# Layer 1's sliding-window attention: the attention sink as a 193rd score column in a fixed tile per group, and the exponentials of a step issued in two halves

## The chip, the cores and the metric

The kernel runs on one core of one Trainium2 chip. The metric is the device time of one execution in microseconds (us). Before the change it is 2704.29 us, the median of 3 runs (2703.48 to 2707.02). A difference of about 0.2%, some 5.4 us, is the least that a measurement of this kernel can tell from none.

A core has five engines that run their own instruction queues in order and wait for each other by semaphores: TensorE (PE in the profile; PEld is its weight load), VectorE (DVE), ScalarE (ACT), GpSimd (POOL) and SyncE (SP), which here only issues DMAs. Matmuls write to PSUM, an accumulator memory of 8 banks; everything else lives in SBUF, the on-chip working memory.

## The reference, cut to what matters

The program is one inference step of a two-layer encoder on 2048 prompt frames and 64 sample frames. The change touches only layer 1, a sliding-window attention with 16 query heads over 2 key/value heads. Each chunk of 64 frames reads itself and the two chunks before it, so at most 192 keys. Each head has a learned sink: one more column of the softmax, with a constant score and no value.

```python
def _grouped_attend(q, k, v, valid, scale, bias=None, sinks=None):
    s = jnp.einsum('...qhgd,...khd->...hgqk', q, k).astype(jnp.float32) * scale
    s = jnp.where(valid, s, NEG_INF)
    if sinks is not None:
        hk, g = q.shape[-3], q.shape[-2]
        sk = jnp.broadcast_to(sinks.astype(jnp.float32).reshape(hk, g, 1, 1), s.shape[:-1] + (1,))
        p = jax.nn.softmax(jnp.concatenate([s, sk], axis=-1), axis=-1)[..., :-1]
    return jnp.einsum('...hgqk,...khd->...qhgd', p.astype(v.dtype), v)

def _c_layer(h, pos, cache, pre_g, post_g, w_in, sinks, w_out):
    ...
        o = _band_prompt(q, k, v, C_PAST_CHUNKS, C_SCALE, sinks=sinks)
    ...
    return h + _rms((o * jax.nn.silu(g)) @ w_out, post_g), state
```

## The kernel before

The program runs five phases one after the other: projections of layer 0, its two attentions, its output projection, the projections of layer 1 (phase 4) and, last, `phase5`: layer 1's attention and output projection. Matmuls use a pair of numbers (a high part and a remainder) for each operand, so many tiles come as `hi` and `lo`: `copy` (L211, on ACT) rounds a PSUM tile to its high part, and `lo_of` (L214, on DVE) subtracts that from the PSUM tile for the remainder.

**Units.** `phase5` works in 64 units: 16 blocks of 128 frames, in each two chunks (`ch`), in each two groups (`g`) of 8 heads. A unit holds 4 score pictures `c` of 128 rows (2 heads by 64 frames) by up to 192 keys. Its life, in the methods of `Soft` and `Unit`:

- `score`: 8 matmuls into the PSUM tile `s` (L1697; two banks, a pool of two such tiles used in turn), then on DVE the row maximum (L1699), the smaller of its negative and the negative sink (L1700, into `m[:,1]`), and sink minus maximum (L1701, into `m[:,2]`).
- `exp`: 4 exponentials on ACT with row sums (L1708, 192 columns each), then one small exponential of the 4 sink terms (L1711).
- `divide`: on DVE the sum plus the sink's term (L1715), a reciprocal (L1716), and the product of `P` and it (L1717).
- `turn`: 4 transposes on PE (L1723), the ACT copy (L211), and behind it the DVE remainder (L214). There are two turns in a unit, 128 keys and 64 keys.
- `av`: 4 matmuls with the values into `acc` (L1730). `out`: ACT copies the upper half of `acc` to `tbm` (L211), and two DVE additions (L1818) write `OT`.

**The output projection** runs between them. When a block's four units are out, `gate` multiplies `OT` by the gate on POOL (L1740), copies it to `MM` on ACT (L211), and subtracts for the remainder on POOL (L1747). `pump` then issues the projection's matmuls (L964) in small portions; ACT copies the result to `z` (L211) and sums its squares (L983); POOL and DVE work out the norm's factor (L987, L186 on POOL, L187 and L188 on DVE, L192 to L197 on POOL); DVE scales `z` in two halves (L995), and POOL adds the residual (L1003).

**Order.** Step `n` of the loop interleaves four units: `n+2` is scored (`ahead`), `n` is turned (`cur`), `n+1` is divided (`nxt`) and `n-1` gets its values and goes out (`prv`). The first 8 steps (`NAUTO5`) are left to a scheduler, which orders each engine's queue by a planned timeline; from step 8 on, the queues of PE, DVE, ACT and SP stand as the code is written, and only POOL's is planned. The heart of a step:

```python
for b in range(2):
    ...
        PT, low = cur.turn(*parts[b][:2])
    ...
    pump(RATE5 / 2)
    if low:
        low()
    if b == 0 and prv:
        prv.av()
    if b == 0 and nxt:
        nxt.divide()
    if b == 0 and prv:
        prv.out()
if ahead:
    ahead.exp([0, 1, 2, 3])
```

The sample's 64 frames form two more units (`sample`), which run their own `score`, `exp` and `divide` among the first steps, with tiles from the same pools.

Of the kernel before, what the change touches and what calls it, by code (L numbers as in the profile page):

```python
# [7 lines left out]
F32 = mybir.dt.float32  # L8
# [3 lines left out]
ALU = mybir.AluOpType  # L12
# [98 lines left out]
def kernel(ctx, tc, a, o, upto=5):  # L111
# [1555 lines left out]
    def phase5():  # L1667

        with ExitStack() as st:
# [8 lines left out]
            sink = row_bcast(one, a["c_sinks"], 16, "sink")  # L1678

            ssink = one.tile([128, 8], F32, name="ssink")  # L1680
            nssink = one.tile([128, 8], F32, name="nssink")
            for e in range(2):
                nc.vector.tensor_copy(ssink[e * 64:e * 64 + 64], sink[e * 64:e * 64 + 64].rearrange("p (j e) -> p j e", e=2)[:, :, e])
            nc.vector.tensor_scalar(nssink, ssink, -1.0, None, op0=ALU.mult)
            class Soft:


                def score(self, lhs, widths, w, g):
                    self.w = w
                    js = slice(g * 4, g * 4 + 4)  # L1690
                    s = self.s = ps_s.tile([128, 4, 256], F32, name="s")
                    m = self.m = sc.tile([128, 3, 4], F32, name="m", bufs=4)
                    for c in range(4):
                        o0 = 0
                        for wd, kk in widths:
                            for x in range(2):
                                nc.tensor.matmul(s[:, c, o0:o0 + wd], lhs(c), kk[x], start=(x == 0), stop=(x == 1))  # L1697
                            o0 += wd
                    nc.vector.tensor_reduce(m[:, 0], s[:, :, :w], axis=AX.X, op=ALU.max)  # L1699
                    nc.vector.scalar_tensor_tensor(m[:, 1], m[:, 0], -1.0, nssink[:, js], op0=ALU.mult, op1=ALU.min)  # L1700
                    nc.vector.tensor_tensor(m[:, 2], m[:, 1], ssink[:, js], op=ALU.add)  # L1701

                def exp(self, cs):
                    m, w = self.m, self.w
                    if cs[0] == 0:
                        self.P = pp.tile([128, 4, 192], F32, name="P")
                    for c in cs:
                        nc.scalar.activation(self.P[:, c, :w], self.s[:, c, :w], AF.Exp, bias=m[:, 1, c:c + 1],  # L1708
                                             accum_out=m[:, 0, c:c + 1])
                    if cs[-1] == 3:  # L1710
                        nc.scalar.activation(m[:, 2], m[:, 2], AF.Exp)  # L1711

                def divide(self):
                    m, w = self.m, self.w
                    nc.vector.tensor_tensor(m[:, 0], m[:, 0], m[:, 2], op=ALU.add)  # L1715
                    nc.vector.reciprocal(m[:, 0], m[:, 0])  # L1716
                    nc.vector.tensor_tensor(self.P[:, :, :w], self.P[:, :, :w], m[:, 0, :, None].to_broadcast([128, 4, w]),  # L1717
                                            op=ALU.mult)

                def turn(self, k0, kk):  # L1720
                    t = ps_t.tile([128, 512], F32, name="t")
                    for c in range(4):
                        nc.tensor.transpose(t[:kk, c * 128:c * 128 + 128], self.P[:, c, k0:k0 + kk], ident)  # L1723
                    PT = ppt.tile([128, 2, 512], F32R, name="PT")
                    copy(PT[:kk, 0], t[:kk])
                    return PT, lambda: lo_of(PT[:kk, 1], t[:kk], PT[:kk, 0])
# [163 lines left out]
            def step(n):  # L1890
# [10 lines left out]
                for b in range(2):  # L1901
# [10 lines left out]
                        nxt.divide()  # L1912
                    if b == 0 and prv:
                        prv.out()
                if ahead:
                    ahead.exp([0, 1, 2, 3])
                if prv:
                    us.pop(n - 1)
                    if n % 4 == 0 and n // 4 + 1 in blocks and n > 0:
# [128 lines left out]
```

## Time and profile before

| | |
|---|---|
| median of 3 runs | 2704.29 us |
| the profiled execution: its time, its span (first to last instruction) | 2703.56 us, 2701.8 us |
| mean granted TensorE clock | 0.986 |
| `phase5`, from its first score to the end of the span | 2237 us to 2701.8 us |
| of it planned by the scheduler (8 steps) / in written order (56 steps and the rest) | to some 2300 us / from there |
| a block (4 steps) in the written order, from one matmul to the same one a block later | 25.8 us |

The page of the profile gives the busy time of each engine and the costliest groups of instructions. The timeline lists instructions of one engine in order: start, duration, engine, source line, operation, tiles written and read, and in brackets the idle time ahead of the instruction with what ended it. The table by stretches gives, for each stretch, its length and then the busy time of PE, PEld, DVE, ACT and POOL, the granted clock and the DMAs' share. In the list of waits each row is the waiting engine and line, what it waited for, the sum, the number of times and the longest.

### The profile page before, as it was taken

To read this page: it belongs to the slowest core of one execution; us is meant where nothing else is said; L and a number is where in the kernel's file an instruction comes from. 1 tells how busy PE (TensorE), PEld (TensorE's weight loads), DVE (VectorE), ACT (ScalarE), POOL (GpSimd) and SP (SyncE) were. 2 spreads that over 40 slices of the span, in tenths; PEclk is the share of its full clock that TensorE was granted. 3 is DMA by queue.
4 is the path that set the end of the run, shared out by engine and by line. 5 is a ranking of instruction groups with operands and counts; after the bars stand their busy time and mean duration, and the time that the engine had idled before them with its cause. 6 is when DMAs were issued, how large, how long until landed. Compare 5 with 4: busy or idle time off the path is not lost.

```text
span 2701.8 us, 46285 instructions
## 1 busy us (share of the span) xinstructions
PE 2564.7 (95%) x16160; PEld 2311.6 (86%) x16160; DVE 1602.8 (59%) x4111; ACT 1359.8 (50%) x3516; POOL 502.5 (19%) x970
## 2 busy tenths in 40 slices
PE   6999999999999999999999999899999998989987
PEld 6999999899998888888778887789999997767765
DVE  6553345453227878787668776474214116899996
ACT  4332242422337777777667666443223214766663
POOL 0001000001002323311201333421001000344443
PEclk9999999999999999999899999999999998999999
DMA  7546443737537666661478776566426349466552
GB/s 241 169 152 209 125 152 115 253 105 226 165 103 206 181 180 191 168 165 48 169 210 191 204 203 185 177 238 209 148 76 191 105 101 235 98 143 132 132 123 74
DMA packets 416760, 438.89 MB, mean 162 GB/s; under 512 B 116224, under 2 KB 343368, under 8 KB 413296
## 3 DMA queue, kind: packets, MB, share of 16 engines
q1 hardware_dynamic: 416528, 435.93, 55.9%
q8 instruction: 129, 2.11, 0.3%
q14 instruction: 103, 0.84, 0.1%
HBM read 283.78 MB, written 157.09 MB: 163 GB/s over the span
## 4 chain that ended last, share of the span: by engine, by line
PE 72%; DVE 14%; ACT 6%; DMA 4%; issue 2%; POOL 1%; SPq 0%; ACTq 0%; DVEq 0%; POOLq 0%
PE pm L237 38%; PE proj L964 8%; PE s L683 6%; PE acc L754 4%; DVE PT L214 3%; PE t L726 3%; PE acc L1228 3%; PE s L1176 2%; PE t L1203 2%; DVE z L995 1%; DVE P L1717 1%; ACT P L702 1%; DVE m L689 1%; POOL x L1003 1%; PE t L1723 1%
## 5 line engine op out<-in xcount | busy, mean ns | idle before, releaser
L237 PE MATMUL pm<-X,W 128*128 128x384 f32 (+2 forms) x4536 | 751.9, 324 | 1.9 <-ACT X L211 1.0
L237 PEld LDWEIGHTS pm<-X,W 128*128 128x128 f32 x4536 | 729.8, 189 | 4.8 <-ACT X L211 1.7
L211 ACT ACTIVATE PT<-t 128x512 fp32r<-128x512 f32 (+3 forms) x704 | 344.9, 504 | 238.0 <-PE t L1203 76.2
L214 DVE SCALAR_TENSOR_TENSOR PT<-t,PT 128x512 fp32r<-128x512 f32 (+4 forms) x688 | 378.8, 569 | 87.7 <-ACT PT L211 83.8
L964 PE MATMUL proj<-Wo,MM 128*128 128x512 f32 (+1 forms) x1440 | 401.3, 408 | 5.6 <-ACT z L211 4.6
L964 PEld LDWEIGHTS proj<-Wo,MM 128*128 128x128 f32 (+1 forms) x1440 | 249.4, 187 | 55.6 <-ACT z L211 8.8
L214 DVE SCALAR_TENSOR_TENSOR ev<-pm,ev 128x256 fp32r<-128x256 f32 (+3 forms) x197 | 98.6, 503 | 334.0 <-ACT ev L430 100.2
L237 PE MATMUL pm<-W,X 128*128 128x256 f32 (+5 forms) x2040 | 281.2, 297 | 0.0
L237 PEld LDWEIGHTS pm<-W,X 128*128 128x128 f32 (+1 forms) x2040 | 272.0, 187 | 1.1
L702 ACT ACTIVATE P<-s,m 128x512 f32<-128x512 f32 (+9 forms) x344 | 209.6, 616 | 33.0 <-DVE m L691 30.4
L683 PE MATMUL s<-KA,Q 128*128 128x512 f32 (+7 forms) x640 | 201.4, 397 | 9.3 <-ACT P L702 8.4
L228 DVE TENSOR_TENSOR W<-R,W 128x768 fp32r<-128x768 f32 (+3 forms) x114 | 116.2, 1055 | 133.0 <-ACT W L227 132.5
L689 DVE TENSOR_REDUCE m<-s 128x1 f32<-128x480 f32 (+7 forms) x216 | 132.4, 613 | 80.6 <-PE s L683 80.3
L726 PE MATMUL t<-ident,P 128*128 128x128 f32 x1088 | 176.4, 276 | 3.4 <-ACT P L702 0.6
L726 PEld LDWEIGHTS t<-ident,P 128*128 128x128 f32 x1088 | 134.6, 141 | 41.6 <-ACT P L702 15.1
L754 PE MATMUL acc<-PT,V 128*128 128x256 f32 x1152 | 156.0, 285 | 6.6 <-DVE OT L763 6.6
L754 PEld LDWEIGHTS acc<-PT,V 128*128 128x128 f32 x1152 | 140.4, 188 | 12.0 <-PE t L726 6.0
L211 ACT ACTIVATE tbm<-acc 64x512 f32<-64x512 f32 (+1 forms) x136 | 77.5, 570 | 117.8 <-PE acc L1730 86.3
L1228 PE MATMUL acc<-PT,V 128*128 128x256 f32 x672 | 111.5, 298 | 6.5 <-DVE OT L1238 4.3
L683 PE MATMUL s<-KR,Q 128*128 128x384 f32 (+6 forms) x320 | 116.2, 363 | 1.2 <-DMA Q<-sQR 1.2
L1180 DVE CUSTOM_DVE_ANT_0 s<-s,bias 128x640 f32<-128x640 f32 (+4 forms) x128 | 95.2, 744 | 35.0 <-PE s L1176 33.5
L227 ACT ACTIVATE W<-R 128x768 fp32r<-128x768 f32 (+3 forms) x114 | 98.2, 909 | 29.6 <-DMA R<-in_ab_w_in_dram 13.0
(238 smaller groups left out, 3907.3 us busy)
## 6 DMA issues: line engine op xcount, KB each, us to landing
Q<-sQA SPq DMA_DIRECT2D x128, 128.0 KB, 3.2
sWO<-W SPq DMA_DIRECT2D x32, 512.0 KB, 3.8
Q<-sQB SPq DMA_DIRECT2D x128, 128.0 KB, 3.2
Wo<-sWO SPq DMA_DIRECT2D x16, 1024.0 KB, 8.8
Q<-sQC SPq DMA_DIRECT2D x64, 256.0 KB, 6.3
R<-in_ab_w_in_dram SPq DMA_DIRECT2D x40, 384.0 KB, 3.9
K<-sKB SPq DMA_DIRECT2D x56, 256.0 KB, 5.4
V<-sVB SPq DMA_DIRECT2D x24, 512.0 KB, 6.6
```

The lines of the kernel that those rows point to most:

```text
L211: nc.scalar.activation(out, in_, AF.Copy)
L214: nc.vector.scalar_tensor_tensor(out, x, scale, hi, op0=ALU.mult, op1=ALU.subtract)
L227: nc.scalar.activation(Wv[:, 0, k0:k1], Rv, AF.Copy)
L228: nc.vector.tensor_tensor(Wv[:, 1, k0:k1], Rv, Wv[:, 0, k0:k1], op=ALU.subtract)
L237: nc.tensor.matmul(ps, lhs(x, k), rhs(y, k), start=(j == 0), stop=(j == n - 1))
L683: nc.tensor.matmul(s[:r, :n], self.Q[:, x, self.qo:self.qo + r], rhs, start=(x == 0), stop=(x == 2))
L689: nc.vector.tensor_reduce(m[:r, j:j + 1], s[:r, :n], axis=AX.X, op=ALU.max)
L702: nc.scalar.activation(self.P[:r, o0:o0 + n], self.s.pop(j)[:r, :n], AF.Exp, bias=self.m[:r, 6:7], accum_out=acc)
L726: nc.tensor.transpose(t[:, b], self.P[:, (b0 + b) * 128:(b0 + b + 1) * 128], ident)
L754: nc.tensor.matmul(acc[:, (i // 2) % 2], H.V[:, b0 + b], PT[:, x, b], start=(b0 + b == 0 and x == 0), stop=(b0 + b == i and x == 1))
L964: nc.tensor.matmul(p, M[:, x, k, :r], W[k][:, y, cs], start=(k == k0 and t == 0), stop=(k == k1 - 1 and t == 2))
L1228: nc.tensor.matmul(acc, self.H.V[:, self.base - self.H.b0 + b], self.PT[:, x, off + b], start=(b == 0 and x == 0), stop=(b == nblk - 1 and ...
```

## The change

The sink becomes part of the score tile. Two fixed PSUM tiles `S_[g]`, one for each group, take the place of the pool's two tiles in turn. Column 192 of each is filled once with the group's sinks; scores are written right-aligned ahead of it, from column `k0 = 192 - w`. The maximum is taken over the scores and the sink together and written with its sign turned; each exponential covers 193 columns, so its row sum holds the sink's term. `nssink`, L1700, L1701, L1711 and L1715 go. `P` gets rows of 193 elements, of which the product covers the 192 without the sink's. And `ahead.exp` moves into the loop over `b`: two of the four exponentials at the end of each half of a step.

```diff
@@ phase5
             ssink = one.tile([128, 8], F32, name="ssink")
-            nssink = one.tile([128, 8], F32, name="nssink")
...
-            nc.vector.tensor_scalar(nssink, ssink, -1.0, None, op0=ALU.mult)
+
+            S_ = [ps_s.tile([128, 4, 256], F32, name=f"s{g}", bufs=1) for g in range(2)]
+            for g in range(2):
+                nc.vector.tensor_copy(S_[g][:, :, 192:193], ssink[:, g * 4:g * 4 + 4, None])
+
             class Soft:
                 def score(self, lhs, widths, w, g):
-                    self.w = w
-                    js = slice(g * 4, g * 4 + 4)
-                    s = self.s = ps_s.tile([128, 4, 256], F32, name="s")
-                    m = self.m = sc.tile([128, 3, 4], F32, name="m", bufs=4)
+                    self.k0 = 192 - w
+                    s = self.s = S_[g]
+                    m = self.m = sc.tile([128, 2, 4], F32, name="m", bufs=4)
                     for c in range(4):
-                        o0 = 0
+                        o0 = self.k0
...
-                    nc.vector.tensor_reduce(m[:, 0], s[:, :, :w], axis=AX.X, op=ALU.max)
-                    nc.vector.scalar_tensor_tensor(m[:, 1], m[:, 0], -1.0, nssink[:, js], op0=ALU.mult, op1=ALU.min)
-                    nc.vector.tensor_tensor(m[:, 2], m[:, 1], ssink[:, js], op=ALU.add)
+                    nc.vector.tensor_reduce(m[:, 1], s[:, :, self.k0:193], axis=AX.X, op=ALU.max, negate=True)
                 def exp(self, cs):
...
-                        self.P = pp.tile([128, 4, 192], F32, name="P")
+                        self.P = pp.tile([128, 4, 193], F32, name="P")
                     for c in cs:
-                        nc.scalar.activation(self.P[:, c, :w], self.s[:, c, :w], AF.Exp, bias=m[:, 1, c:c + 1],
+                        nc.scalar.activation(self.P[:, c, k0:193], self.s[:, c, k0:193], AF.Exp, bias=m[:, 1, c:c + 1],
                                              accum_out=m[:, 0, c:c + 1])
-                    if cs[-1] == 3:
-                        nc.scalar.activation(m[:, 2], m[:, 2], AF.Exp)
                 def divide(self):
-                    m, w = self.m, self.w
-                    nc.vector.tensor_tensor(m[:, 0], m[:, 0], m[:, 2], op=ALU.add)
+                    m, P = self.m, self.P[:, :, self.k0:192]
                     nc.vector.reciprocal(m[:, 0], m[:, 0])
-                    nc.vector.tensor_tensor(self.P[:, :, :w], self.P[:, :, :w], m[:, 0, :, None].to_broadcast([128, 4, w]),
-                                            op=ALU.mult)
+                    nc.vector.tensor_tensor(P, P, m[:, 0, :, None].to_broadcast([128, 4, 192 - self.k0]), op=ALU.mult)
...
@@ step
                     if b == 0 and prv:
                         prv.out()
-                if ahead:
-                    ahead.exp([0, 1, 2, 3])
+                    if ahead:
+                        ahead.exp([2 * b, 2 * b + 1])
```

By the change the line numbers move by two to four: the maximum is L1701 after it, the reciprocal L1713, the product L1714, the transposes L1719, the values L1726, the additions to `OT` L1814; the exponentials stay L1708. In the rows below, `s_25807` and `s_25808` are the two fixed tiles of groups 0 and 1.

The order of the queues shows the change in three places. The first is DVE's queue in the written order, a step and a half around the scaling of `z` (L995). Before:

```order
L995 SCALAR_TENSOR_TENSOR z<-z,rs,g_post 128x512
L1699 TENSOR_REDUCE m<-s 128x4
L1700 SCALAR_TENSOR_TENSOR m<-m,nssink 128x4
L1701 TENSOR_TENSOR m<-m,ssink 128x4
L187 TENSOR_SCALAR rs<-rs 128x1
L188 TENSOR_SCALAR rs<-rs 128x1
L214 SCALAR_TENSOR_TENSOR PT<-t,PT 128x512
L1715 TENSOR_TENSOR m<-m 128x4
L1716 RECIPROCAL m<-m 128x4
L1717 TENSOR_TENSOR P<-P,m 128x768
L1818 TENSOR_TENSOR OT<-acc,tbm 64x4x64 x2
L214 SCALAR_TENSOR_TENSOR PT<-t,PT 64x512
```

The same stretch of DVE's queue after the change:

```order
L995 SCALAR_TENSOR_TENSOR z<-z,rs,g_post 128x512
L1701 TENSOR_REDUCE m<-s_25807 128x4
L187 TENSOR_SCALAR rs<-rs 128x1
L188 TENSOR_SCALAR rs<-rs 128x1
L214 SCALAR_TENSOR_TENSOR PT<-t,PT 128x512
L1713 RECIPROCAL m<-m 128x4
L1714 TENSOR_TENSOR P<-P,m 128x4x192
L1814 TENSOR_TENSOR OT<-acc,tbm 64x4x64 x2
L214 SCALAR_TENSOR_TENSOR PT<-t,PT 64x512
```

Three small instructions of each unit are gone from it, and nothing has changed places.

The second place is ACT's queue in the written order, from the copy of `z` to the end of the next step. Before:

```order
L211 ACTIVATE z<-proj 128x512
L1708 ACTIVATE P,m<-s,m 128x192 x4
L1711 ACTIVATE m<-m 128x4
L211 ACTIVATE MM<-OT 128x1024
L211 ACTIVATE PT<-t 128x512
L983 ACTIVATE sq,ss_26701<-z 128x512
L211 ACTIVATE tbm<-acc 64x512
L211 ACTIVATE PT<-t 64x512
L1708 ACTIVATE P,m<-s,m 128x192 x4
L1711 ACTIVATE m<-m 128x4
```

The same stretch of ACT's queue after the change:

```order
L211 ACTIVATE z<-proj 128x512
L1708 ACTIVATE P,m<-s_25808,m 128x193 x2
L211 ACTIVATE MM<-OT 128x1024
L211 ACTIVATE PT<-t 128x512
L983 ACTIVATE sq,ss_26631<-z 128x512
L211 ACTIVATE tbm<-acc 64x512
L1708 ACTIVATE P,m<-s_25807,m 128x193 x2
L211 ACTIVATE PT<-t 64x512
L1708 ACTIVATE P,m<-s_25807,m 128x193 x2
```

Two of a unit's exponentials now stand between the copy of `tbm` and the copy of the second turn (`PT<-t 64x512`); two stay behind it; the small one is gone.

The third place is DVE's queue among the planned steps, around the maxima of the sample's first unit. Before:

```order
L1699 TENSOR_REDUCE m<-s 128x4 x2
L214 SCALAR_TENSOR_TENSOR ev<-proj,ev 128x384
L1700 SCALAR_TENSOR_TENSOR m<-m,nssink 128x4 x2
L1701 TENSOR_TENSOR m<-m,ssink 128x4 x2
L1715 TENSOR_TENSOR m<-m 128x4
L1716 RECIPROCAL m<-m 128x4
L1717 TENSOR_TENSOR P<-P,m 128x768
```

The same place of DVE's queue after the change:

```order
L1701 TENSOR_REDUCE m<-s_25807 128x4
L1701 TENSOR_REDUCE m<-s_25808 128x4
L1713 RECIPROCAL m<-m 128x4
L1714 TENSOR_TENSOR P<-P,m 128x4x192
L1713 RECIPROCAL m<-m 128x4
L1714 TENSOR_TENSOR P<-P,m 128x4x192
L214 SCALAR_TENSOR_TENSOR ev<-proj,ev 128x384
```

Here the scheduler has planned anew: the remainder of the last query projection (`ev<-proj`) has moved from between the maxima and what follows them to behind the products.

More of the change, by code (lines that the diff above doesn't have):

```diff
@@ L1698, in score @@
                             o0 += wd
-                    nc.vector.tensor_reduce(m[:, 0], s[:, :, :w], axis=AX.X, op=ALU.max)
-                    nc.vector.scalar_tensor_tensor(m[:, 1], m[:, 0], -1.0, nssink[:, js], op0=ALU.mult, op1=ALU.min)
-                    nc.vector.tensor_tensor(m[:, 2], m[:, 1], ssink[:, js], op=ALU.add)
+                    nc.vector.tensor_reduce(m[:, 1], s[:, :, self.k0:193], axis=AX.X, op=ALU.max, negate=True)
                 def exp(self, cs):
-                    m, w = self.m, self.w
+                    m, k0 = self.m, self.k0
                     if cs[0] == 0:
-                        self.P = pp.tile([128, 4, 192], F32, name="P")
+                        self.P = pp.tile([128, 4, 193], F32, name="P")
                     for c in cs:
-                        nc.scalar.activation(self.P[:, c, :w], self.s[:, c, :w], AF.Exp, bias=m[:, 1, c:c + 1],
+                        nc.scalar.activation(self.P[:, c, k0:193], self.s[:, c, k0:193], AF.Exp, bias=m[:, 1, c:c + 1],
                                              accum_out=m[:, 0, c:c + 1])
-                    if cs[-1] == 3:
-                        nc.scalar.activation(m[:, 2], m[:, 2], AF.Exp)
                 def divide(self):
-                    m, w = self.m, self.w
-                    nc.vector.tensor_tensor(m[:, 0], m[:, 0], m[:, 2], op=ALU.add)
+                    m, P = self.m, self.P[:, :, self.k0:192]
                     nc.vector.reciprocal(m[:, 0], m[:, 0])
-                    nc.vector.tensor_tensor(self.P[:, :, :w], self.P[:, :, :w], m[:, 0, :, None].to_broadcast([128, 4, w]),
-                                            op=ALU.mult)
+                    nc.vector.tensor_tensor(P, P, m[:, 0, :, None].to_broadcast([128, 4, 192 - self.k0]), op=ALU.mult)
                 def turn(self, k0, kk):
@@ L1722, in turn @@
                     for c in range(4):
-                        nc.tensor.transpose(t[:kk, c * 128:c * 128 + 128], self.P[:, c, k0:k0 + kk], ident)
+                        nc.tensor.transpose(t[:kk, c * 128:c * 128 + 128], self.P[:, c, self.k0 + k0:self.k0 + k0 + kk], ident)
                     PT = ppt.tile([128, 2, 512], F32R, name="PT")
```

## The prediction

> **What bounds the kernel now.** The page comes first, for the share of each engine, and then the table by stretches, cut at the three parts of `phase5`: the planned steps, the written order and the end (columns: stretch, length, busy time of PE, PEld, DVE, ACT, POOL, granted clock).
>
> ```profile
> PE 2564.7 (95%) x16160; PEld 2311.6 (86%) x16160; DVE 1602.8 (59%) x4111; ACT 1359.8 (50%) x3516; POOL 502.5 (19%) x970
> ```
> ```profile
> 2237.00:2300.00 63.00, 54.24 (x274) 42.26 (x273) 41.40 (x95) 34.67 (x120) 7.97 (x4) 0.81 0.86 218
> 2300.00:2640.00 340.00, 313.23 (x1705) 240.86 (x1704) 307.89 (x587) 228.85 (x740) 132.15 (x220) 1.00 0.57 126
> ```
>
> Over the whole run PE is the bound and DVE has air. In the written order that is not so: PE is idle for 340 - 313.23 = 26.8 us, and DVE, busy for 307.89, is nearly as full. The list of waits in the same stretch says whose fault it is:
>
> ```profile
> PE t L1723 <- DVE P L1717: 26.2, 24, 1.7
> DVE PT L214 <- ACT PT L211: 15.2, 14, 1.5
> ```
>
> Nearly all of PE's idle time is a wait of the transposes for the product on DVE. So PE's work, 313 us here, is the floor, and nothing can be won in this stretch beyond 26.8 us. The groups of DVE in it (mean ns of one behind the busy time) show what the change removes:
>
> ```profile
> L1717 DVE TENSOR_TENSOR P<-P,m 128x768 f32<-128x768 f32 x49 | 47.2, 963 | 1.7
> L1700 DVE SCALAR_TENSOR_TENSOR m<-m,nssink 128x4 f32<-128x4 f32 x54 | 25.7, 476 | 1.8
> L1715 DVE TENSOR_TENSOR m<-m 128x4 f32<-128x4 f32 x54 | 25.5, 472 | 0.0
> L1701 DVE TENSOR_TENSOR m<-m,ssink 128x4 f32<-128x4 f32 x54 | 8.8, 163 | 1.8
> ```
>
> Three instructions on 4 columns take 60.0 us together. L1701 needs 163 ns for as many elements as the other two; their means of 476 and 472 are a few very long ones. The timelines of DVE, POOL and PE over one block show why:
>
> ```profile
> 2509.79 0.69 DVE L214 SCALAR_TENSOR_TENSOR PT<-t,PT 128x512 fp32r<-128x512 f32 x1 [1.07 <-ACT PT L211]
> 2510.40 1.37 DVE L1715 TENSOR_TENSOR m<-m 128x4 f32<-128x4 f32 x1
> ...
> 2512.01 0.96 DVE L1717 TENSOR_TENSOR P<-P,m 128x768 f32<-128x768 f32 x1
> ...
> 2514.37 2.39 DVE L995 SCALAR_TENSOR_TENSOR z<-z,rs,g_post 128x512 f32<-128x512 f32 x1
> 2516.68 0.94 DVE L1699 TENSOR_REDUCE m<-s 128x4 f32<-128x768 f32 x1
> ...
> 2517.94 0.68 DVE L214 SCALAR_TENSOR_TENSOR PT<-t,PT 128x512 fp32r<-128x512 f32 x1
> 2518.54 0.15 DVE L1715 TENSOR_TENSOR m<-m 128x4 f32<-128x4 f32 x1
> 2518.72 0.18 DVE L1716 RECIPROCAL m<-m 128x4 f32<-128x4 f32 x1
> 2518.94 0.96 DVE L1717 TENSOR_TENSOR P<-P,m 128x768 f32<-128x768 f32 x1
> ...
> 2522.93 1.58 DVE L1700 SCALAR_TENSOR_TENSOR m<-m,nssink 128x4 f32<-128x4 f32 x1
> ...
> 2524.95 0.15 DVE L187 TENSOR_SCALAR rs<-rs 128x1 int32<-128x1 int32 x1 [0.24 <-POOL rs L186]
> ```
> ```profile
> 2509.35 2.39 POOL L1747 TENSOR_TENSOR MM<-OT,MM 128x1024 fp32r<-128x1024 f32 x1 [6.01 <-ACT MM L211]
> 2513.81 2.40 POOL L1740 TENSOR_TENSOR OT<-OT,G 128x1024 f32<-128x1024 f32 x1 [2.07 <-DVE OT L1818]
> 2522.10 2.38 POOL L1003 TENSOR_TENSOR x<-z,x 128x1024 f32<-128x1024 f32 x1 [5.90 <-DVE z L995]
> ```
> ```profile
> 2520.04 0.63 PE L1723 MATMUL t<-ident,P 128*128 128x128 f32 x4 [1.65 <-DVE P L1717]
> 2527.34 0.63 PE L1723 MATMUL t<-ident,P 128*128 128x128 f32 x4 [0.65 <-DVE P L1717]
> ```
>
> Each of POOL's three long instructions ends with one DVE instruction: L1715 at 2511.77 (POOL at 2511.74), L1700 at 2524.51 (2524.48), and L995, which runs its 0.56 after POOL's end at 2516.21. DVE stands still while POOL works whenever it comes to an instruction with two SBUF inputs; L214 and L1699, which read PSUM, go on. And each block has two PE waits, (a) 1.65 and (b) 0.65, together 2.30.
>
> **The change, part by part.** *Wait (a).* I follow its chain back to ACT, whose timeline at the start of the block reads:
>
> ```profile
> 2504.70 0.60 ACT L211 ACTIVATE tbm<-acc 64x512 f32<-64x512 f32 x1 [1.92 <-PE acc L1730]
> 2505.32 0.59 ACT L211 ACTIVATE PT<-t 64x512 fp32r<-64x512 f32 x1
> 2506.02 0.60 ACT L211 ACTIVATE z<-proj 128x512 f32<-128x512 f32 x1
> 2506.51 0.41 ACT L1708 ACTIVATE P<-s,m 128x192 f32<-128x192 f32 x1
> ...
> 2508.10 0.22 ACT L1711 ACTIVATE m<-m 128x4 f32<-128x4 f32 x1
> 2508.20 1.08 ACT L211 ACTIVATE MM<-OT 128x1024 fp32r<-128x1024 f32 x1
> 2509.14 0.61 ACT L211 ACTIVATE PT<-t 128x512 fp32r<-128x512 f32 x1
> ```
>
> An exponential starts every 0.40 ((2508.10 - 2506.51) / 4). After the change: `tbm` 2504.70, two exponentials from 2505.32, the second turn's copy at 2506.12, `z` 0.50 later at 2506.62, exponentials from 2507.11, `MM` at 2507.91. That is 0.29 earlier, out of L1711 and the short idle time ahead of `z`. So L1747 starts on POOL at 2509.06 and ends at 2511.45, and L214 starts at 2509.50. Behind that L1715 is gone; the reciprocal has one input and need not wait, but the product L1714 has two and waits to 2511.48 in L1715's place. It ends at 2512.44, before the change at 2512.97: 0.53 won, most of it from the order, little from the stall. The additions, L1740 and the stalled L995 move up by the same 0.53. Then L1700 and L1701 are missing between L1699 and L214 (2517.94 - 2516.68 = 1.26 becomes 0.94, the maximum's own time): 0.32. And L1715, start to start with L1716: 0.19. Sum 1.04, and (a) falls from 1.65 to 0.61.
>
> *Wait (b).* From the release of (a) the chain runs: product, additions, L214, L995, L1003 on POOL for 2.38, its norm instructions up to L186, then L187, L188, L214, L1716, L1717. The 1.58 of L1700 lies under L1003 and gains nothing when it goes, for L187 waits for POOL anyway. Only L1715's 0.19 is on the chain: (b) becomes 0.46.
>
> A block thus gains 1.04 + 0.19 = 1.23 of 2.30, a share of 0.53. The other waits of this kind are shorter chains of the same links, and the last one in the written order is
>
> ```profile
> 2648.97 0.63 PE L1723 MATMUL t<-ident,P 128*128 128x128 f32 x4 [2.50 <-DVE P L1717]
> ```
>
> so I take the share for all: 0.53 x (26.8 + 2.50) = **15.6 us**. That is the first term.
>
> *The planned steps*, 2237 to 2300, have 63 - 54.24 = 8.8 us of PE idle time, and the longest piece stands at the sample:
>
> ```profile
> 2262.99 0.48 PE L1697 MATMUL s<-KCS,QS 128*128 128x128 f32 x1 [3.29 <-ACT P L1708]
> 2261.22 0.42 ACT L1708 ACTIVATE P<-s,m 128x192 f32<-128x192 f32 x1 [2.97 <-DVE m L1700]
> ```
>
> PE waits for exponentials, and these for L1700, which stands behind two maxima and an `ev` remainder. After the change the exponential waits for its own maximum alone, one maximum (0.94) and the remainder earlier, up to 1.5. But the same score tile now has to serve the group's next unit, and the whole stretch is planned anew, so the cost is unknown on both sides: at best all 8.8 us go, at worst as much again comes. I take a gain of **1 us**, near the row's 0.94.
>
> *Costs at nothing, and their cover.* A 193rd column in L1708 and L1699: one in 192 of 0.41 and four in 768 of 0.94, under 0.01 each. The two copies of sinks into PSUM stand on DVE ahead of this row, in its idle 2.56:
>
> ```profile
> 2238.44 0.56 DVE L214 SCALAR_TENSOR_TENSOR ev<-proj,ev 128x384 fp32r<-128x384 f32 x1 [2.56 <-ACT ev L1573]
> ```
>
> The moved exponentials delay the copy of the second turn by 0.8, and its L214 with it. Cover: at (a) `tbm` ends at 2516.89, the new exponentials wait for the maximum until 2517.09, the copy ends near 2518.5, and DVE comes to that L214 only after its additions, near 2519.7. In the fourth step DVE would wait some 0.5, but there it idles 1.07 for the next copy anyway (the row at 2509.79).
>
> *Two unknowns.* That L1714 waits for POOL is not seen before the change, since L1715 always stood ahead of it; its group's mean of 963 shows no stall. The nearest rows on the lock are these, a product that had started first:
>
> ```profile
> 2289.20 0.96 DVE L1717 TENSOR_TENSOR P<-P,m 128x768 f32<-128x768 f32 x1
> ```
> ```profile
> 2285.86 1.27 POOL L1740 TENSOR_TENSOR OTs<-OTs,G 128x512 f32<-128x512 f32 x1 [184.84 <-DVE OTs L1853]
> 2289.35 1.94 POOL L1747 TENSOR_TENSOR MM<-OTs,MM 128x512 fp32r<-128x512 f32 x1 [2.22 <-PE acc L1730]
> ```
>
> POOL needed 0.67 more than for as large a tile and ended 1.13 after the product: it had been held. So the product holds what POOL needs, and I take it that POOL holds it against the product too. The Trainium skill's page "SBUF — State Buffer", section "SBUF: two separate sides", says why: GpSimd and a VectorE instruction with two SBUF inputs share one port pair, which goes to the first comer for its whole instruction. By that rule the stall moves to the next two-input instruction instead of going, which speaks against much of this change; the trace agrees as far as its rows go.
>
> The other unknown is the rows of 193 words in `P`: every second one starts at an odd word. Bounds: nothing, or at most as much again as L1717's 0.96 for each of three products in a block's chains; I take nothing, since each row is still one run of 192. The skill's "Vector Engine (DVE) Microarchitecture Reference", section "Measured stream behaviour on trn2", gives 1.30 ns a column instead of 1.05 where pairs start on odd words. If that held for half the rows, it would be an estimated 0.1 us a product and some 3 us in all; no row here shows such a case.
>
> **Sum.** 2703.56 - 15.6 - 1.0 = 2687.0 for the profiled execution; the median shown is 0.7 above it, less than is worth adding.
>
> **The rivals.**
> 1. *Both waits vanish*: L1714 does not stall on POOL, or the re-plan fills the sample's gap as well. Without its stall L1714 ends some 1.2 earlier than counted; (a) is gone with 0.6 to spare, which (b) takes. Gain 29.3 + 1, time 2673. For it: no L1717 was ever long. Against it: the held POOL row.
> 2. *The re-plan gives it back.* In the planned steps the granted clock is 0.81 on average. If PE idled 8.8 us more there, and the low-clock time (0.19 x 63 = 12 us lost) grew by a third, some 13 us would be spent, time 2700. For it: the fixed tile ties the sample's unit to its group. Against it: fewer instructions stand in each chain.
> 3. *Slower: the second turn's copy becomes the bound.* Two exponentials and the copy end 1.4 after `tbm`, DVE's additions 0.85 after it. Wherever DVE isn't late, it then stands some 0.55, and up to 0.8 where the exponentials wait for a maximum. At 0.8 in all four steps, 3.2 a block against the 2.0 that DVE is spared (four times 0.51), PE's waits grow by 1.2 a block instead: 2703.6 + 13 x 1.2 = 2719. It decides from the point where the copy ends after L1814 on average. Against it: in three steps of four DVE runs behind (2527 against a `tbm` at 2524).
> 4. *The change doesn't do what it says*: the waits move whole to the product, leaving only L1715's 0.19 twice a block: 2703.6 - 13 x 0.38 = 2699.
>
> **How the numbers follow.** My forecast has 0.58, rival 1 has 0.17, rival 2 0.10, rival 3 0.07, rival 4 0.08. A measurement can tell about 0.2%, 5.4 us, from no change; below 2698.9 counts as faster. The forecast and rival 1 lie below, rivals 2 and 4 on the line's far side, with a few hundredths below it: faster 0.80, same 0.13, slower 0.07. The range goes from rival 1's 2673 to rival 2's 2700 and leaves out rival 3 and the tails, some 0.17.
>
> **What would show it.** In the profile after: L1714 with a few long ones of about 2.0 to 2.3 once a block, as long as POOL's L1743 (formerly L1747) lasts; L1003 without any stalled DVE instruction beside it, but L187 still waiting for L186; blocks of 24.6 us instead of 25.8; PE waits of about 0.6 and 0.45 for L1714. Wrong would be: no long L1714 (rival 1), L214 waiting for the `PT` copy in more than one step of four (rival 3), or a planned stretch longer than 63 us (rival 2).

## The result and the profile after

| | before | after |
|---|---|---|
| median | 2705.57 us | 2685.54 us |
| lowest and highest of 4 runs each | 2703.48, 2707.02 | 2682.74, 2691.66 |
| ratio of the times, 95% interval | | 0.993 (0.9911 to 0.9949) |
| the profiled execution: span | 2701.8 us | 2689.9 us |
| a block of 4 steps in the written order | 25.8 us | 24.2 us |

The change is faster by 0.7%, 20 us, and the interval lies clear of no change. The profiled execution of after is the slowest of its four, 6.1 us above the median; its first score falls at 2245.3 us instead of 2237.7, in phases that the change does not touch. So I compare from the first score on. Cut there, and at the first and the thirteenth of POOL's full-size L1003, the two profiles stand like this:

| stretch of `phase5`, us | before | after |
|---|---|---|
| first score to the first L1003 (the planned steps and two blocks) | 109.0 | 108.4 |
| twelve blocks, L1003 to L1003 | 304.3 | 285.6 |
| from there to the end | 50.7 | 50.6 |

Nearly all of the gain that the profile shows lies in the written order: 18.7 us in twelve blocks, 1.56 a block. The page of after, and the table by stretches at the cuts of before, of which the first begins 8 us ahead of after's first score (columns: stretch, length, busy time of PE, PEld, DVE, ACT, POOL, granted clock, DMA share and rate):

```profile
PE 2573.6 (96%) x16160; PEld 2318.3 (86%) x16160; DVE 1554.1 (58%) x3914; ACT 1349.4 (50%) x3450; POOL 502.6 (19%) x970
```
```profile
2237.00:2300.00 63.00, 58.26 (x295) 48.50 (x294) 36.25 (x62) 31.27 (x106) 4.31 (x3) 0.74 0.85 233
2300.00:2640.00 340.00, 332.72 (x1786) 252.93 (x1785) 275.31 (x444) 229.76 (x716) 140.27 (x224) 1.00 0.55 129
```

In the written order PE's idle time went from 26.8 to 340 - 332.72 = 7.3 us, and DVE has 32.6 us less to do (307.89 to 275.31). The list of waits of that stretch:

```profile
DVE PT L214 <- ACT PT L211: 25.2, 32, 1.7
DVE rs L187 <- POOL rs L186: 23.4, 12, 2.6
...
PE t L1719 <- DVE P L1714: 5.8, 13, 0.9
...
PEld proj L964 <- ACT z L211: 3.7, 14, 0.3
```

PE waits for the product 5.8 us where it waited 26.2. DVE now waits itself, for copies of ACT and for the root's first value from POOL. The last row is new, there is none such before: the weight loads (PEld) of the projection wait for ACT to empty the projection's PSUM tile, 14 times at 3.7 / 14 = 0.26 us. Where POOL's hold went (the time in which a DVE instruction stands still until a POOL instruction is through), the groups of DVE show:

```profile
L1714 DVE TENSOR_TENSOR P<-P,m 128x768 f32<-128x768 f32 (+2 forms) x56 | 66.3, 1184 | 1.9
L995 DVE SCALAR_TENSOR_TENSOR z<-z,rs,g_post 128x512 f32<-128x512 f32 (+1 forms) x26 | 39.5, 1518 | 0.1
```

The product's mean is 1184 ns where L1717 had 963. The timelines of DVE, POOL and PE over one block:

```profile
2506.89 0.69 DVE L214 SCALAR_TENSOR_TENSOR PT<-t,PT 128x512 fp32r<-128x512 f32 x1 [1.16 <-ACT PT L211]
2507.49 0.17 DVE L1713 RECIPROCAL m<-m 128x4 f32<-128x4 f32 x1
2507.70 1.95 DVE L1714 TENSOR_TENSOR P<-P,m 128x768 f32<-128x768 f32 x1
2509.57 0.84 DVE L1814 TENSOR_TENSOR OT<-acc,tbm 64x256 f32<-64x256 f32 x2
2510.44 0.68 DVE L214 SCALAR_TENSOR_TENSOR PT<-t,PT 64x512 fp32r<-64x512 f32 x1
2511.05 2.38 DVE L995 SCALAR_TENSOR_TENSOR z<-z,rs,g_post 128x512 f32<-128x512 f32 x1
2513.35 0.95 DVE L1701 TENSOR_REDUCE m<-s 128x4 f32<-128x772 f32 x1
...
2515.02 0.96 DVE L1714 TENSOR_TENSOR P<-P,m 128x768 f32<-128x768 f32 x1
...
2517.37 0.73 DVE L995 SCALAR_TENSOR_TENSOR z<-z,rs,g_post 128x512 f32<-128x512 f32 x1
...
2521.02 0.15 DVE L187 TENSOR_SCALAR rs<-rs 128x1 int32<-128x1 int32 x1 [2.05 <-POOL rs L186]
```
```profile
2506.45 2.37 POOL L1743 TENSOR_TENSOR MM<-OT,MM 128x1024 fp32r<-128x1024 f32 x1 [5.40 <-ACT MM L211]
2510.49 2.39 POOL L1736 TENSOR_TENSOR OT<-OT,G 128x1024 f32<-128x1024 f32 x1 [1.66 <-DVE OT L1814]
2518.19 2.37 POOL L1003 TENSOR_TENSOR x<-z,x 128x1024 f32<-128x1024 f32 x1 [5.31 <-DVE z L995]
```
```profile
2498.96 0.63 PE L1719 MATMUL t<-ident,P 128*128 128x128 f32 x4 [0.40 <-DVE P L1714]
2499.35 1.63 PE L964 MATMUL proj<-Wo,MM 128*128 128x512 f32 x6
...
2504.06 0.60 PE L1719 MATMUL t<-ident,P 128*128 128x128 f32 x4
2504.68 2.36 PE L964 MATMUL proj<-Wo,MM 128*128 128x512 f32 x9
...
2516.12 0.63 PE L1719 MATMUL t<-ident,P 128*128 128x128 f32 x4
...
2523.19 0.63 PE L1719 MATMUL t<-ident,P 128*128 128x128 f32 x4 [0.35 <-DVE P L1714]
```

L1714 at 2507.70 stands until POOL's L1743 is through (2508.82) and ends 0.83 us behind it; L1713 ahead of it, with one input, takes its usual 0.17. Wait (b) is still there, 0.35 at 2523.19 and 0.40 a block earlier; wait (a), at 2516.12, shows no idle time. But the projection's first matmul at 2504.68 starts 0.62 behind the first of its four transposes, where the one at 2499.35 needs 0.39. This **pause** is the 0.26 of the PEld row; the modelled ends of the matmuls hide it from PE's idle time.

### The profile page after: what moved, and what is told of

It is laid out like the page before. It is cut to its first block, busy times and chain, and to the rows that moved or that the text cites. A ratio compares the mean times of both kernels' runs of the same rounds, so it can differ in the third digit from the quotient of the medians.

```text
span 2689.9 us, 46026 instructions
## 1 busy us (share of the span) xinstructions
PE 2573.6 (96%) x16160; PEld 2318.3 (86%) x16160; DVE 1554.1 (58%) x3914; ACT 1349.4 (50%) x3450; POOL 502.6 (19%) x970
## 4 chain that ended last, share of the span: by engine, by line
PE 74%; DVE 12%; ACT 6%; DMA 4%; issue 2%; POOL 1%; SPq 0%; ACTq 0%; DVEq 0%; POOLq 0%
PE pm L237 39%; PE proj L964 8%; PE s L683 6%; PE acc L754 4%; PE t L726 3%; DVE PT L214 3%; PE acc L1228 3%; PE s L1176 2%; PE t L1203 2%; DVE P L1714 2%; DVE z L995 1%; ACT P L702 1%; DVE m L689 1%; PE acc L1726 1%; ACT PT L211 1%
## 5 line engine op out<-in xcount | busy, mean ns | idle before, releaser
L214 DVE SCALAR_TENSOR_TENSOR PT<-t,PT 128x512 fp32r<-128x512 f32 (+4 forms) x688 | 378.4, 568 | 101.6 <-ACT PT L211 98.0
L214 DVE SCALAR_TENSOR_TENSOR ev<-pm,ev 128x256 fp32r<-128x256 f32 (+3 forms) x197 | 98.6, 502 | 339.0 <-ACT ev L430 99.3
L1708 ACT ACTIVATE P<-s,m 128x193 f32<-128x193 f32 (+2 forms) x264 | 106.8, 413 | 15.6 <-DVE m L1701 12.8
```

The source lines that it names most:

```text
L214: nc.vector.scalar_tensor_tensor(out, x, scale, hi, op0=ALU.mult, op1=ALU.subtract)
L1708: nc.scalar.activation(self.P[:, c, k0:193], self.s[:, c, k0:193], AF.Exp, bias=m[:, 1, c:c + 1], accum_out=m[:, 0, c:c + 1])
```

## The experiments

All block figures below are means over five steady blocks of the profiled run, from L1003 to L1003; (a) and (b) are PE's idle times in them, and the pause is the time by which the projection's first matmul starts late (the pitch from a transpose to the matmul behind it, above its usual 0.03).

My first theory: the gain comes from the three DVE instructions that are gone from the two chains, and the hold of POOL moves to the product. Rivals: the split of the exponentials makes it (A), the fixed tiles and the planned steps make it (B), or the small instructions' holds were the cost (C).

### One half of the change at a time

The column without the split:

```diff
-                    if ahead:
-                        ahead.exp([2 * b, 2 * b + 1])
+                if ahead:
+                    ahead.exp([0, 1, 2, 3])
```

> The changed kernel with the four exponentials of a step back behind its second turn; the fixed tiles and the 193rd column stay. My theory (the gain comes from the DVE instructions that are gone from both chains, so the split is worth little): blocks of 24.2 to 24.6 us against 24.24 in the changed kernel and 25.80 before, the waits of PE on the product at most 0.8 us a block, time 2685 to 2691. Rival A (the split of the exponentials makes most of the gain): blocks of 25.2 us or more, waits of 1.4 us a block or more, time 2698 or more.

Measured: 2687.67 us, ratio 0.9936 (0.9918 to 0.9955), blocks of 24.47. PE's timeline in this kernel, the two waits of one block:

```profile
2523.26 0.63 PE L1719 MATMUL t<-ident,P 128*128 128x128 f32 x4 [0.58 <-DVE P L1714]
2530.33 0.63 PE L1719 MATMUL t<-ident,P 128*128 128x128 f32 x4 [0.39 <-DVE P L1714]
```

Waits 0.58 and 0.39 a block, 0.17 more together than expected, and no pause. And the split in the kernel before, nothing else (`ahead.exp` as in the change, four instructions as before):

> The kernel before with nothing but the split of the exponentials. My theory: the exponentials start earlier only where ACT is free earlier, and the three small DVE instructions stay on both chains, so the blocks keep 25.3 to 25.8 us (before: 25.80), the waits 1.8 to 2.3 us, time 2697 to 2706. Rival A: blocks of 24.8 us or less, waits at most 1.3 us, time 2692 or less.

Measured: 2701.38 us, ratio 0.999 (0.998 to 1.0001), not to be told from no change; blocks of 25.54. PE's timeline in this kernel, the two waits of one block, and from its list of waits (2300 to 2620) the row that before hasn't:

```profile
2523.00 0.63 PE L1723 MATMUL t<-ident,P 128*128 128x128 f32 x4 [1.16 <-DVE P L1717]
2530.30 0.63 PE L1723 MATMUL t<-ident,P 128*128 128x128 f32 x4 [0.63 <-DVE P L1717]
```
```profile
PEld proj L964 <- ACT z L211: 3.2, 13, 0.3
```

The split takes 0.48 off (a) and adds the pause of 0.26: net 0.25 a block with or without the column (25.79 to 25.54, 24.47 to 24.22). Rival A falls; the column makes 1.32 of the 1.57.

### The three instructions put back, in three forms

Three small instructions at the places of L1700, L1701 and L1715, on a tile that nobody reads; here with two SBUF inputs:

```diff
                     nc.vector.tensor_reduce(m[:, 1], s[:, :, self.k0:193], axis=AX.X, op=ALU.max, negate=True)
+                    js = slice(g * 4, g * 4 + 4)
+                    gh = self.gh = sc.tile([128, 3, 4], F32, name="gh", bufs=4)
+                    nc.vector.scalar_tensor_tensor(gh[:, 0], m[:, 1], -1.0, ssink[:, js], op0=ALU.mult, op1=ALU.min)
+                    nc.vector.tensor_tensor(gh[:, 1], gh[:, 0], ssink[:, js], op=ALU.add)
...
+                    nc.vector.tensor_tensor(self.gh[:, 2], m[:, 0], self.gh[:, 1], op=ALU.add)
                     nc.vector.reciprocal(m[:, 0], m[:, 0])
```

> The changed kernel with three small DVE instructions of two SBUF inputs (4 elements a row) added where the three removed ones stood; nothing reads what they write. My theory (instructions on the chain, whatever their inputs, and the place at which POOL's lock strikes): blocks of 25.0 to 25.8 us, both waits back at 1.2 to 2.2 us a block together, the product L1714 no longer held (below 1.2 us in every step), time 2694 to 2703. Rival C (the lock of POOL on the removed ones was the cost): the same here, 25.3 us or more.

Measured: 2699.36 us, ratio 0.9982 (0.9973 to 0.999), blocks of 25.43, (a) 1.05 and (b) 0.60. Theory and rival C agree here. With tiles, column and no L1711 the blocks are only 0.11 below those of the split alone (25.54), so these three together are worth little in the written order. The holds are back on the small ones, and the product (L1719 in this kernel) has none, as its groups of DVE show (the last figures are busy time, mean ns of one, idle time ahead):

```profile
L1719 DVE TENSOR_TENSOR P<-P,m 128x768 f32<-128x768 f32 (+2 forms) x54 | 50.4, 933 | 1.9
L1704 DVE SCALAR_TENSOR_TENSOR gh<-m,ssink 128x4 f32<-128x4 f32 x54 | 27.1, 502 | 1.8
L1717 DVE TENSOR_TENSOR gh<-m,gh 128x4 f32<-128x4 f32 x54 | 25.4, 471 | 0.0
```

With one input each, by `nc.vector.tensor_scalar(..., op0=ALU.mult)`:

> As the run with two inputs, but the three added instructions have one SBUF input each, so that POOL does not hold them. My theory: most of the loss is back all the same, since each is 0.15 to 0.25 us on the chain; blocks of 24.7 to 25.4 us, at most 0.4 below the run with two inputs, time 2690 to 2699. Rival C (the lock): blocks within 0.3 us of the changed kernel's 24.24, time 2685 to 2689, at least 0.8 us a block below the run with two inputs.

Measured: 2700.42 us, ratio 0.9985 (0.9976 to 0.9994), blocks of 25.47. The run does not tell what it was made for, because its premise was wrong: these are held as well, by this kernel's groups of DVE:

```profile
L1703 DVE TENSOR_SCALAR gh<-m 128x4 f32<-128x4 f32 x54 | 27.5, 509 | 1.8
L1716 DVE TENSOR_SCALAR gh<-m 128x4 f32<-128x4 f32 x54 | 25.8, 478 | 0.0
L1704 DVE TENSOR_SCALAR gh<-gh 128x4 f32<-128x4 f32 x54 | 9.2, 170 | 1.8
```

The Trainium skill's page "VectorE: DVE Perf Modes", section "Mode 2×_2P — use both read ports for one tensor", says that a `tensor_scalar` with its one source in SBUF, fp32 too, can use both read ports for it. The means of 509 and 478 ns, against 170 for the one that stands behind another, show such an instruction meeting POOL's hold; that the ports are the reason, no run shows. So the same again with `nc.vector.reciprocal`, which had not been long in any trace:

> As the runs with three instructions added, but with reciprocals, which POOL did not hold in any trace so far (0.156 to 0.169 us in the changed kernel, never longer), so the lock stays at the product L1714 and only instruction time comes back. My theory (instruction time on the chain): blocks of 25.0 to 25.5 us, within 0.4 of the 25.4 of the other two, time 2695 to 2701. Rival C (the lock on small instructions ahead of the product): blocks of 24.2 to 24.7 us, time 2685 to 2690. Rival D (half of each: the place of the lock and the instruction time): 24.7 to 25.0.

Measured: 2696.1 us, ratio 0.997 (0.9958 to 0.9981), blocks of 25.08, (a) 0.67, (b) 0.63, the pause 0.25. The groups of DVE in this kernel:

```profile
L1718 DVE TENSOR_TENSOR P<-P,m 128x768 f32<-128x768 f32 (+2 forms) x55 | 62.5, 1136 | 1.9
L1704 DVE RECIPROCAL gh<-gh 128x4 f32<-128x4 f32 x55 | 9.8, 178 | 1.8
L1703 DVE RECIPROCAL gh<-m 128x4 f32<-128x4 f32 x55 | 9.7, 177 | 1.8
L1716 DVE RECIPROCAL gh<-m 128x4 f32<-128x4 f32 x55 | 9.1, 166 | 0.0
```

Now the hold is at the product, as in the changed kernel, and three instructions of 0.17 us cost 0.85 of the 1.21 us a block that the first form cost. The place of the hold is the other 0.36. Instruction time is the larger part, but not all; rival C is right about the rest.

### The hold itself

POOL's subtraction as a memset, in the kernel before:

```diff
-                nc.gpsimd.tensor_tensor(MM[:, 1, :, :r], OT[:, :, :r], MM[:, 0, :, :r], op=ALU.subtract)
+                nc.gpsimd.memset(f(MM[:, 1, :, :r]), 0.0)
```

> The kernel before with POOL's subtraction L1747 replaced by a memset to zero: it leaves out the low part of the layer's projection input. One of POOL's three long instructions in a block no longer holds a small DVE instruction. My theory: the held L1715 (up to 1.74 us) is 0.15 us in every step, but the wait ahead of it is where DVE had time, so blocks lose at most 0.6 us of 25.8 and the time is 2697 to 2705. Rival C: the wait of 1.65 us a block falls to 0.6 or less, blocks 24.8 or less, time 2690 or less.

Measured: 2688.8 us, ratio 0.9946 (0.9934 to 0.9959), blocks of 24.57. My theory fell, rival C's numbers came. The group of L1715 and PE's waits of one block in this kernel:

```profile
L1715 DVE TENSOR_TENSOR m<-m 128x4 f32<-128x4 f32 x56 | 9.9, 177 | 0.0
```
```profile
2510.95 0.63 PE L1723 MATMUL t<-ident,P 128*128 128x128 f32 x4 [0.43 <-DVE P L1717]
2518.23 0.63 PE L1723 MATMUL t<-ident,P 128*128 128x128 f32 x4 [0.60 <-DVE P L1717]
```

L1715's mean falls from 472 ns to 177, and (a) from 1.65 to about 0.45: the edit was worth 1.2 of it, as much as a held L1715 takes above a free one (1.37 and 0.15 in the rows of before). (The memset also takes 0.95 us of POOL instead of 2.39 and waits for no copy of ACT; neither this run nor the next parts that from the hold.) The same edit in the changed kernel:

> The changed kernel with POOL's subtraction L1743 replaced by a memset to zero: it leaves out the low part of the layer's projection input. In the kernel before the same edit took the blocks from 25.79 to 24.57 us, as the wait (a) fell from 1.65 to 0.45. My theory (after the change the held product L1714 costs PE nothing, since (a) is 0 already): no long L1714 from it, blocks of 24.15 to 24.25, within 0.1 of 24.22, time 2683 to 2688 (the tail may save 2 us besides). Rival (the hold still sets the block): blocks of 23.9 or less, time 2680 or less.

Measured: 2673.91 us, ratio 0.9885 (0.9867 to 0.9904), blocks of 23.63. My theory fell a second time: with (a) at 0 in the profile, POOL's subtraction and its hold still cost 0.59 a block. The groups of DVE in this kernel:

```profile
L1714 DVE TENSOR_TENSOR P<-P,m 128x768 f32<-128x768 f32 (+2 forms) x55 | 52.4, 953 | 1.9
L187 DVE TENSOR_SCALAR rs<-rs 128x1 int32<-128x1 int32 (+1 forms) x15 | 2.3, 153 | 26.6 <-POOL rs L186 26.5
```

L187 still waits as long for POOL, yet (b) is gone. (The projection's weight loads now wait twice a block for ACT to empty its tile, some 0.5 together.) The timelines of after, above, suggest the link: the held L1714 delays L1814, that delays L1736 on POOL (2510.49, 0.08 behind L1814's end), that holds L995 to 2513.43, and over the second L995, L1003, L186 and L187 the delay reaches the product of (b). I read this path from the rows; no run cut it at another link but the next one.

### The later root

```diff
-            y = rstd_of(ss[:r, 0:1], r, DM, eng)
+            t = rstd_start(ss[:r, 0:1], r, DM, eng)
+            early = J.split and eng is nc.gpsimd
+            if early:
+                yield
+            y = rstd_of(ss[:r, 0:1], r, DM, eng, t)
             if not J.last:
-                yield
+                if not early:
+                    yield
                 yield
                 yield
```

(`rstd_start` is L186 alone, `rstd_of` then does the rest, and `J.split` is set in `phase5`; these lines of the edit aren't shown.)

> The changed kernel with the reciprocal root of the projection split, so that DVE's L187 is written one step behind POOL's L186 for which it waits 2.05 us in each block. My theory of the wait (b), that this stall on DVE alone sets it: no wait of L187 over 0.3 us, the 0.35 us of PE a block gone, blocks of 23.8 to 24.0 us, time 2679 to 2684. Rival: the wait is set by the step itself, so L214 then waits for PT instead; blocks stay at 24.1 to 24.3, time 2684 to 2688.

Measured: 2672.29 us, ratio 0.989 (0.9874 to 0.9905), below the interval of the change: **it beats both kernels** and leaves nothing out. Blocks of 23.67, better than I expected. Its table by stretches and its list of PE's waits, from 2300 to 2620:

```profile
2300.00:2620.00 320.00, 316.69 (x1719) 242.80 (x1718) 275.09 (x431) 221.61 (x694) 146.12 (x221) 1.00 0.56 133
```
```profile
PE t L1731 <- DVE P L1726: 1.8, 2, 0.9
```

No steady block has a wait of PE for the product any more. The hold hasn't gone: with L187 out of the way a second product of each block comes to L1003 (L1015 in this kernel) and stands, in DVE's and POOL's timelines:

```profile
2504.86 1.69 DVE L1726 TENSOR_TENSOR P<-P,m 128x768 f32<-128x768 f32 x1
```
```profile
2503.34 2.38 POOL L1015 TENSOR_TENSOR x<-z,x 128x1024 f32<-128x1024 f32 x1 [5.30 <-DVE z L1007]
```

Of the 0.55 a block, 0.35 is (b) and 0.06 were gaps too short to be listed; the rest I can't assign. Of the 13.3 us between the medians, the profiles show 6.1 in the twelve blocks (279.5), 1.4 in the end (49.2) and 3.2 in the planned steps (105.2). The last isn't shown to be the root's: over that stretch the granted clock was 0.84 in the profile of the change and 0.90 in this one. The same edit in the kernel before:

> The kernel before with the later root alone. There L187 waits at most 0.25 us for POOL, since the held L1700 stands ahead of it, so my theory (the wait (b) of before is made by the three instructions and the held one, and L187's stall matters only after the change) gives blocks of 25.6 to 25.9 us, waits (a) 1.65 and (b) 0.5 to 0.65, time 2701 to 2705. Rival (the root is as good before the change): blocks of 25.2 or less, time 2697 or less.

Measured: 2700.11 us, ratio 0.9985 (0.9972 to 0.9997), blocks of 25.18. PE's timeline in this kernel has one wait of a block left:

```profile
2521.07 0.63 PE L1735 MATMUL t<-ident,P 128*128 128x128 f32 x4 [1.67 <-DVE P L1729]
```

(a) is as it was, (b) is gone whole, and my theory with it: the root was a link of (b) before the change too. There L187's own stall was short (0.24), since the held L1700 ran out the same POOL time ahead of it; but with L187 and L188 it put 0.67 us between the starts of L1701 and L214 (2524.54 to 2525.21), where this kernel's timeline of DVE has 0.08:

```profile
2525.56 0.16 DVE L1713 TENSOR_TENSOR m<-m,ssink 128x4 f32<-128x4 f32 x1
2525.64 0.68 DVE L221 SCALAR_TENSOR_TENSOR PT<-t,PT 128x512 fp32r<-128x512 f32 x1
```

In the profile the twelve blocks are 5.3 us shorter than before (299.0), the planned steps 2.3 and the end 1.1 longer; the medians differ by 4.7.

### The planned steps, and the pause

Four planned steps instead of eight (`NAUTO5 = 4`) in the changed kernel:

> The changed kernel with four planned steps instead of eight; steps 4 to 7 then stand in written order. My theory (the gain is made in the written order, the planner's steps are about even): within 4 us of the changed kernel, 2682 to 2690, blocks of 24.2 unchanged, the time from the first score to step 8 within 4 us. Rival B (the fixed tiles made the planned steps better or worse): 2692 or more, or 2680 or less, by that stretch alone.

Measured: 2686.25 us, ratio 0.9936 (0.9923 to 0.9948), blocks of 24.23, and 109.4 us from the first score to the first L1003 against 108.4. Rival B finds nothing in the planned steps. (The fixed tiles stay in this run; what they are worth in the written order is the 0.11 above, with the column and L1711.)

The exponentials split one and three, to let ACT come to `z` earlier:

```diff
-                        ahead.exp([2 * b, 2 * b + 1])
+                        ahead.exp([1, 2, 3] if b else [0])
```

In the changed kernel:

> The changed kernel with the split one and three, nothing else. My theory: the 0.26 us pause of the projection goes, blocks 23.9 to 24.1 instead of 24.22, time 2681 to 2685; if the pause covered part of the next wait for the product, that wait grows by as much as 0.25 and the blocks stay at 24.2.

Measured: 2681.57 us, ratio 0.9921 (0.9902 to 0.994), overlapping the change's interval; blocks of 24.24. PE's timeline in this kernel, the two waits of one block:

```profile
2504.81 0.63 PE L1719 MATMUL t<-ident,P 128*128 128x128 f32 x4 [0.36 <-DVE P L1714]
2511.88 0.63 PE L1719 MATMUL t<-ident,P 128*128 128x128 f32 x4 [0.39 <-DVE P L1714]
```

The PEld row is gone, and a wait (a) of 0.36 stands in its place. So the pause had covered it: (a) did not vanish in the changed kernel, PE merely came later. With the later root as well:

> The later root and the exponentials split one and three instead of two and two. In the traces with two and two the first projection matmul behind one turn of each block starts 0.29 us behind the last transpose instead of 0.03, because ACT empties the one projection bank behind two exponentials. My theory (that pause is real and comes from the second of them): the pitch is 0.03 to 0.05 again, blocks fall from 23.67 to 23.4 us (23.35 to 23.5), time 2666 to 2671. Rival: ACT is no wait here, blocks stay at 23.6 to 23.7, time 2671 to 2674.

Measured: 2678.43 us, ratio 0.9899 (0.9882 to 0.9916). The pause is gone as I said, and the blocks stay at 23.65 as the rival said, with (a) at 0.34. Its median is 6 us longer than with the later root alone, with the two intervals overlapping. In the profiles the first score to the first L1003 took 111.0 us against 105.2, at a granted clock of 0.85 against 0.90, so the 6 us aren't shown to come from the split.

| kernel | median us | block | (a) | (b) | pause |
|---|---|---|---|---|---|
| before | 2705.57 | 25.79 | 1.65 | 0.63 | 0 |
| split alone | 2701.38 | 25.54 | 1.16 | 0.61 | 0.26 |
| three back, two inputs | 2699.36 | 25.43 | 1.06 | 0.60 | 0.25 |
| three back, one input | 2700.42 | 25.47 | 1.08 | 0.62 | 0.25 |
| three back, reciprocals | 2696.10 | 25.08 | 0.67 | 0.63 | 0.25 |
| column alone | 2687.67 | 24.47 | 0.58 | 0.39 | 0 |
| the change | 2685.54 | 24.22 | 0 | 0.36 | 0.27 |
| the change, four planned steps | 2686.25 | 24.23 | 0 | 0.37 | 0.25 |
| the change, one and three | 2681.57 | 24.24 | 0.35 | 0.39 | 0 |
| before, no remainder | 2688.80 | 24.57 | 0.45 | 0.61 | 0 |
| before, later root | 2700.11 | 25.18 | 1.66 | 0 | 0 |
| the change, no remainder | 2673.91 | 23.63 | 0 | 0.03 | 0.51 |
| the change, later root | 2672.29 | 23.67 | 0 | 0 | 0.28 |
| the change, later root, one and three | 2678.43 | 23.65 | 0.34 | 0 | 0 |

## Why the prediction was right, and which terms were small

**The mechanism held.** The bound was the one named: two waits a block for the product on DVE. The hold moved to L1714 once a block, until L1743 is through (1.94 to 1.98 us in the steady blocks, forecast 2.0 to 2.3), and L187 kept waiting for L186. One reason was too narrow: POOL holds not only instructions with two SBUF inputs, for a `TENSOR_SCALAR` with one was held too; that the reciprocal ahead of L1714 runs through (0.17 us) came out, but not for the reason that it has one input. What the prediction did not see is a cost of the split, the pause (below).

**Wait (a): 1.65, forecast 0.61, measured 0.35** (as it stands where no pause covers it). The runs price each term of the sum of 1.04:

| term | forecast | measured | from |
|---|---|---|---|
| ACT earlier, L1711 gone (with the tiles and the column) | 0.29 | 0.33 | 1.65 to 1.16 and the pause of 0.26, then 1.16 to 1.05 |
| the hold at the product instead of L1715 | 0.24 | 0.38 | 1.05 to 0.67 |
| L1700, L1701 and L1715, their own time | 0.51 | 0.59 | 0.67 and 0.25, to 0 and 0.27 and gaps of 0.06 |
| sum | 1.04 | 1.30 | 1.65 to 0.35 |

No step failed; each term was small. (The forecast's 0.53 for L1714's end is split here into ACT's 0.29 and the hold's 0.24.) The largest error is the second: I let the held product end 0.99 behind POOL, and it ended 0.83 behind.

**Wait (b): 0.65, forecast 0.46, measured 0.35 to 0.39.** That L1700's hold is under L1003 and gains nothing was right: moving the holds about left (b) between 0.60 and 0.63. The instructions' own time is 0.25, not L1715's 0.19 alone.

**A block: 24.6 forecast, 24.2 measured, a gain of 1.57 instead of 1.23.** In twelve blocks that is 4.1 us, about the 3.4 by which the gain of 20.0 exceeds the forecast of 16.6. That the time itself, 2685.5 us, lies within 1.5 us of the 2687.0 on record is in part luck: the median of before, with its fourth run, is 2.0 above the 2703.56 from which the sum starts. (The profiled execution of after took 2691.66; its first score came 7.6 us later than that of before.)

**The planned steps: 1 us forecast, 0.6 in the profile** (109.0 to 108.4 us, first score to first L1003). In that stretch PE's idle time fell from 9.4 us (109.0 - 99.65) to 5.4 (108.4 - 103.02), but the granted clock fell too, from 0.89 to 0.84, so what the new plan is worth at an equal clock isn't shown. Among the changed kernel's variants the stretch took 104.0 to 106.8 us where the clock in it was 0.90 to 0.92 (one and three, no remainder, later root, two of the three with instructions put back) and 108.4 to 111.0 where it was 0.83 to 0.85. What sets the low-clock time is open, and a difference of a few us between two of these kernels can be this alone.

**Costs at nothing.** The column: the reduction over 772 elements takes 0.95 against 0.94. The odd rows of `P`: an L1714 that is not held takes 0.96 like L1717, so of the 0.1 us that the prediction estimates from the Trainium skill for odd words, nothing shows. The delayed second copy: DVE's waits for `PT` copies rose from 15.2 to 25.2 us, but on an engine that had become early. What I did not count is that the exponentials also stand ahead of `z`, which empties the projection's only PSUM tile: the pause.

**The rivals.** The first (both waits vanish) needed an L1714 that doesn't stall; the stall came, (b) stayed, and (a) is covered rather than gone. The run of the change without POOL's subtraction comes near what that rival describes: hardly a wait for the product left, and 2673.9 us against its 2673. The second, the plan that gives the gain back, came by half in the profile: the clock did fall in the planned steps, but PE idled less, not more, and the stretch did not grow. The third, slower by the second copy, did not happen, though the sign named for it did: L214 waits for copies 32 times in 14 blocks of four steps, more than one step of four, but DVE had the time. The fourth, that the waits move whole, is refuted by (a).

## What to carry to other kernels

A tiny instruction on a full engine costs its own time (0.15 to 0.18 us here) on every chain through it, and where another engine holds it, the hold goes to the next instruction of its kind when it is removed, not away. Price both by putting the instruction back in a form that is held and in one that is not. When a wait closes, look for the next link of the same chain, on whichever engine, and for a pause that only a late start shows: here one `yield` between two instructions of the root took the blocks from 24.2 to 23.7 us.

## What the runs showed of the hardware that I had not expected

- One-input `TENSOR_SCALAR` instructions on 4 fp32 columns were held by POOL's long instructions just as two-input ones were (means of 509 and 502 ns), while reciprocals were not (at most 0.18 us in the run with three of them, where 57 lie wholly within such an instruction).
- A held instruction finishes sooner after its release than it takes alone: the product 0.83 us behind POOL's end instead of 0.96, L995 0.55 instead of 0.73. Whether part of its work is done while it stands, no run shows.
- The low clock lasted while PE was busy. Of the changed kernel's planned steps (stretch, length, PE's busy time, and the granted clock as the third number from the end):

```profile
2268.00:2284.00 16.00, 15.53 (x59) 12.27 (x59) 11.21 (x20) 9.55 (x34) 0.00 (x0) 0.50 0.81 282
2284.00:2300.00 16.00, 15.54 (x56) 11.29 (x56) 11.60 (x20) 9.67 (x33) 4.31 (x3) 0.50 0.45 83
```

By its modelled ends PE worked for 31.1 of 32 us at half the clock. The Trainium skill's page "TensorE: Matmul & The Clock Gate", section "Part 1: The HAM clock gate", lets the clock rise after some 3.4 us of sustained work; these rows don't agree, and no run here shows why.
